# Narrow products of a hybrid decoder step placed side by side in TensorE's array

## The chip, the cores and the metric

The kernel runs on one core of a Trainium2 chip. The metric is the device time of one execution in microseconds (us). Engines are called as the profile calls them: PE is TensorE's matmul, PEld its weight load, DVE is VectorE, ACT is ScalarE, POOL is GpSimd, SP is SyncE, which issues most DMAs.

## What is computed

One inference step of a decoder layer for 1024 prompt tokens and for 32 new tokens (8 sequences of 4, each with 1024 past tokens). Cut to what the change touches:

```python
mod = silu(c) @ w_ada + b_ada                       # 9 conditions: the prompt's and the 8 sequences'
shift, scale, gate = split(mod, 3)
# indexer, new tokens: relu of each of 4 heads, weighted and summed over the heads
s = einsum('bqhd,bsd->bqhs', qi, ki); scores = einsum('bqhs,bqh->bqs', relu(s), w)
# retention of the prompt, in 8 chunks of 128 tokens, 8 heads of 64
scores = einsum('bihd,bjhd->bhij', q, k) * dmat
# output projection with the gate, residual and final norm
x = x + gate[:, None, :] * (merged @ w_out)
y = rms_norm(x, g_final)
```

All of it is in 32-bit floats. Products whose operands are plain float32 (F32) run as two passes of the array, so that the profile has two matmuls and two weight loads for each; products that are written as three terms (high, low) in float32r (F32R) run in one pass each.

## The kernel before

The kernel is one program of some 20,000 instructions without loops at run time. It is written with tiles; a planner orders the instructions of each engine by their priority (the order in which the program was written) and by a simulated timeline, and sets the waits. `issue_after` ties an instruction behind another one on its engine. The stages follow each other in time:

- Until 152 us: norms, modulation, the indexer's projections and scores. The new tokens' index scores end in the **index sums** (L822 to L826): for each half G of the sequences, `wsel[:, G]` (128 rows, 32 columns) is multiplied with `RL[G]` in two runs of 512 columns, and both G add up in one PSUM tile of 32 rows and 1024 columns. One ACT copy brings it to `SCS`, on which the search for the 256 best keys works.
- 152 to 516 us: **retention** (`pair`, for four pairs p of heads), its projections on PE, and on DVE and ACT the search (31 rounds, tied to the projections by `marks`). The products of keys and queries (L596 to L601) run for two groups g of four chunks. `two()` takes two PSUM tiles `pb` of the three that there are, one for each head i; head i uses rows 64i to 64i+63 of the array and all 128 columns, so that the products of two heads can run side by side.
- 516 to 700 us: scores of the new tokens against gathered keys (`past_scores`), beside the projections of keys and values.
- 700 to 817 us: the new tokens' values (`values`, gathers of 512 KB on POOL's queue, products L1100) beside, for p = 0 to 3, `silu_rows(p)` (a projection of 72 matmuls), `gates(12 + p)` (another) and **`gate_rows(p)`**: two loads from `w_ada`, 32 narrow matmuls in four column parts of the array (L212), an ACT copy to `ga`, a product with the 32 columns of `C_SEL` that adds up the four parts (L994), an ACT copy of 9 rows to `gr`, and a DMA of these to DRAM (`GD`). Loads of projection weights and of `w_ada` share the two buffers `ws` in turn; `project` takes the weights split before and begins with `prefetch` of the next: load, ACT cast to `wh` (L204), difference to `wl` on DVE or POOL (L205), each with two buffers as well. A `ws` buffer of projection weights is free after the split, one of `w_ada` after its L212.
- 817 to 972 us: attention of the prompt, filled up with the products of retention's rows (L1006 to L1008).
- 972 to 1023 us: merging, output j by output j; the new tokens' columns of each go to `MS` as high and low parts. `load_wo(0)` loads the four blocks of `w_out`'s first half into `wst` (4 buffers) and splits them.
- 1023 us to the end: **output projection**. `part(t, sl, ...)` takes one tile of 128 prompt tokens (t < 8), 24 F32R matmuls of 512 columns for each half of the outputs, or the 32 new tokens (t = 8): 16 F32R matmuls of 512 columns for each half, with 32 or 64 columns of the array used. The order is (8, 0, 1) first halves, then their second halves, then tiles 2 to 7 one by one; `final` norms a tile and writes it.

Of the kernel before, what the change touches and what calls it, by code (L numbers as in the profile page):

```python
# [117 lines left out]
def _hybrid_step(ctx, tc, A, outs, dbg):  # L118
# [406 lines left out]
    def pair(rp, RC, O, SD, p, rows):  # L525
# [70 lines left out]
        for g in (0, 1):  # L596
            px = two()
            together([lambda c=c, i=i: nc.tensor.matmul(px[i][:, 128 * c:128 * c + 128],
                                                        kT[head[i], 512 * g + 128 * c:512 * g + 128 * c + 128],
                                                        qT[head[i], 512 * g + 128 * c:512 * g + 128 * c + 128], start=True, stop=True)  # L600
                      for c in range(4) for i in (0, 1)])  # L601
# [94 lines left out]
    with ExitStack() as s1:  # L696
# [4 lines left out]
        with ExitStack() as s2:  # L701
# [120 lines left out]
            for G in (0, 1):  # L822
                for n0 in (0, 512):
                    nc.tensor.matmul(x[:NS, n0:n0 + 512], wsel[:, G], RL[G][:, n0:n0 + 512], start=(G == 0), stop=(G == 1))
                nc.tensor.matmul(xn[:NS, :NS], wsel[:, G], RL[G][:, PAST:], start=(G == 0), stop=(G == 1))
            nc.scalar.copy(SCS[:, :PAST], x[:NS])  # L826
# [159 lines left out]
    def gate_rows(tl, p):  # L986
# [4 lines left out]
        ga = tl.tile([128, 256], F32, name="ga", bufs=1)  # L991
        nc.scalar.copy(ga, x[:, :256])
        x = pj()
        nc.tensor.matmul(x[:NS, :256], C[:, C_SEL:C_SEL + 32], ga, start=True, stop=True)  # L994
        gr = tl.tile([9, 256], F32, name="gr", bufs=1)
        nc.scalar.copy(gr, x[:9, :256])
        (nc.scalar if p == 3 else nc.sync).dma_start(GD[:, 256 * p:256 * p + 256], gr)
# [144 lines left out]
    yrh, yrl = rows_in(rm, YR)  # L1142
    for p in range(4):
        silu_rows(tl, p)
        gates(tl, (12 + p,))
        gate_rows(tl, p)
    nc.sync.dma_start(zs, by_pair(ZD))
    nc.vector.tensor_tensor(YS, YS, zs, op=OP.mult)
    tl_.close()
    hs_.close()  # L1150
# [172 lines left out]
    MS = fp.tile([128, KT, 2, NS], F32R, name="MS")  # L1323
    WO = [[fp.tile([128, KT, 512], F32R, name=f"wo{a}0") for a in "hl"]]

    def load_wo(q, js):

        for j in js:
            w = fp.tile([128, 4, 256], F32, name="wst", bufs=4)
            g, c = divmod(j, 2)  # L1330
            nc.sync.dma_start(w, A["w_out"][0][512 * g:512 * g + 512, 512 * q + 256 * c:512 * q + 256 * c + 256].rearrange("(k p) f -> p k f", p=128))
            h, l = [a[:, 4 * g:4 * g + 4, 256 * c:256 * c + 256] for a in WO[q]]
# [3 lines left out]
    for n_, j in enumerate(line):  # L1336
# [4 lines left out]
        def use_a(c, sl, x):  # L1341
# [4 lines left out]
            if c == 2:  # L1346
                parts((MS[:, j, 0], MS[:, j, 1]), t[:, T:])
# [25 lines left out]
    def part(t, sl, i, xo, xr, sv):  # L1373
# [14 lines left out]
        else:  # L1388
            for k in range(KT):
                if k > 0:  # L1390
                    nc.tensor.matmul(x[:NS], MS[:, k - 1, 0], wl[:, k - 1], start=False, stop=False)
                    if k == KT - 1:
                        nc.tensor.matmul(x[:NS], MS[:, k, 0], wl[:, k], start=False, stop=False)
                nc.tensor.matmul(x[:2 * NS], MS[:, k].rearrange("p a c -> p (a c)"), wh[:, k], start=(k == 0), stop=(k == KT - 1))
            nc.scalar.copy(g, x[NS:2 * NS])
            nc.vector.tensor_tensor(g, g, x[:NS], op=OP.add)
# [16 lines left out]
    for ts in ((8, 0, 1), (2,), (3,), (4,), (5,), (6,), (7,)):  # L1413
        cuts = halves if ts != (7,) else [slice(0, 512), slice(512, 768), slice(768, 1024)]
        tiles = {}
        for i, sl in enumerate(cuts):
            for t in ts:
                if i == 0:
                    xo, xr = op_.tile([128, D], F32, name="xo", bufs=3), urow()[:, :D]
                    tiles[t] = xo, xr, op_.tile([128, 4], F32, name="sv", bufs=4)  # L1420

                    with tc.issue_after(asked[line[-1]].ins):
                        nc.sync.dma_start(*((xr, xp[128 * t:128 * t + 128]) if t < 8 else (xr[:NS], xs)))
# [26 lines left out]
```

## Time and profile before

| | us |
|---|---|
| time, median of 3 runs | 1127.78 (1127.6 to 1127.87) |
| the profiled execution's own time | 1127.94 |
| span in the profile | 1126.2 |
| PE busy (share of the span) | 1087.8 (97%) |
| PEld busy | 988.8 (88%) |
| DVE busy | 678.6 (60%) |
| ACT busy | 472.4 (42%) |
| POOL busy | 226.6 (20%) |
| DMA moved, mean | 183.51 MB, 163 GB/s |

The span is the time from the first to the last instruction of the program in one profiled execution; that execution's own time is 1.7 us longer. Matmuls are pipelined: the next one starts before the last one's end, so a group's cost is read from starts, or from the busy time of the group, not from the mean duration of one. A time that follows "idle before" is time in which the engine waited, with the event that ended it.

### The profile page before, as it was taken

What the parts mean: (1) busy time and instruction counts of PE and PEld (TensorE: products, weight loads), DVE (VectorE), ACT (ScalarE), POOL (GpSimd) and SP (SyncE); (2) the same over time, 40 slices, a digit from 0 to 9 for tenths busy, and PEclk for the clock granted to TensorE, in tenths of its full rate; (3) what the DMA queues carried; (4) which work ended last, traced back from release to release, by engine and by line L of the source; (5) the groups of instructions that cost most, each with busy time, mean ns of one, the idle gap of its engine ahead of it and who ended that gap; (6) DMA issues with size and microseconds to landing.
All of it is one profiled execution on the core that took longest, in us unless ns stands there. A gap on an engine that the chain in (4) does not pass through costs nothing.

```text
span 1126.2 us, 20190 instructions
## 1 busy us (share of the span) xinstructions
PE 1087.8 (97%) x7978; PEld 988.8 (88%) x7978; DVE 678.6 (60%) x1649; ACT 472.4 (42%) x914; POOL 226.6 (20%) x194
## 2 busy tenths in 40 slices
PE   6989999999999999989999999989999999999997
PEld 5779889899999999989999999767889888898886
DVE  6775348698878969996222222201367777488645
ACT  6574345455554644232343323211335666343111
POOL 0012006114321211022321212232013333100000
PEclk9999999999999999999999999999999999999999
DMA  9933335155243434414877666586897511456321
GB/s 311 234 90 95 101 98 152 45 172 142 78 151 111 134 92 152 134 42 136 294 240 242 186 203 204 185 299 225 272 328 274 185 61 41 151 159 230 121 90 56
DMA packets 153909, 183.51 MB, mean 163 GB/s; under 512 B 18565, under 2 KB 124749, under 8 KB 152726
## 3 DMA queue, kind: packets, MB, share of 16 engines
q1 hardware_dynamic: 143718, 145.96, 41.6%
q0 software_dynamic: 9856, 35.66, 9.6%
q8 instruction: 63, 1.03, 0.4%
q10 hardware_dynamic: 240, 0.61, 0.1%
q14 instruction: 32, 0.26, 0.1%
HBM read 137.23 MB, written 41.17 MB: 158 GB/s over the span
## 4 chain that ended last, share of the span: by engine, by line
PE 83%; DVE 8%; DMA 5%; issue 2%; ACT 1%; SPq 1%; DVEq 0%; ACTq 0%
PE pj L218 15%; PE pj L219 15%; PE pj L220 15%; PE po L1229 3%; PE pj L1006 3%; PE pj L1007 3%; PE pj L1008 3%; PE pj L1384 3%; PE pj L1385 3%; PE pj L1386 3%; PE str L1072 3%; PE tr L1212 2%; PE lg L1190 2%; DMA x<-in_w_ada 1%; PE sx L1051 1%
## 5 line engine op out<-in xcount | busy, mean ns | idle before, releaser
L218 PE MATMUL pj<-hh,wh 128*128 128x352 f32 (+1 forms) x1168 | 383.2, 328 | 1.6 <-DVE qs L724 1.1
L219 PE MATMUL pj<-hl,wh 128*128 128x352 f32 (+1 forms) x1168 | 378.8, 324 | 0.0
L220 PE MATMUL pj<-hh,wl 128*128 128x352 f32 (+1 forms) x1168 | 378.6, 324 | 0.0
L218 PEld LDWEIGHTS pj<-hh,wh 128*128 128x128 f32 x1168 | 219.8, 188 | 11.4 <-issue 8.5
L219 PEld LDWEIGHTS pj<-hl,wh 128*128 128x128 f32 x1168 | 220.3, 189 | 3.4 <-issue 2.5
L220 PEld LDWEIGHTS pj<-hh,wl 128*128 128x128 f32 x1168 | 219.7, 188 | 1.5 <-issue 0.8
L842 DVE TENSOR_SCALAR_CACHE_REDUCE eq<-sc,cand 128x896 bf16<-128x896 f32 (+4 forms) x155 | 135.8, 876 | 2.6
L204 ACT CAST wh<-ws 128x1024 fp32r<-128x1024 f32 (+1 forms) x65 | 61.0, 941 | 128.0 <-PE pj L219 73.1
L205 DVE TENSOR_TENSOR wl<-ws,wh 128x1024 fp32r<-128x1024 f32 (+1 forms) x48 | 58.2, 1213 | 62.5 <-ACT wh L204 62.4
L1199 POOL TENSOR_SCALAR lg<-lg,st 128x1024 f32<-128x1024 f32 (+7 forms) x64 | 47.9, 754 | 119.4 <-DVE st L1198 106.5
L205 POOL TENSOR_TENSOR wl<-ws,wh 128x1024 fp32r<-128x1024 f32 x17 | 41.7, 2450 | 143.2 <-ACT wh L204 121.0
L1197 ACT ACTIVATE lg<-lg,st 128x1024 f32<-128x1024 f32 (+7 forms) x64 | 49.5, 774 | 29.9 <-DVE st L1196 27.8
L1074 DVE COPY kt<-str 128x512 f32<-128x512 f32 x32 | 22.1, 690 | 62.1 <-PE str L1072 58.4
L1384 PE MATMUL pj<-woh,MH 128*128 128x512 f32 (+1 forms) x136 | 51.2, 377 | 0.0
L1385 PE MATMUL pj<-wol,MH 128*128 128x512 f32 (+1 forms) x136 | 51.2, 377 | 0.0
L1386 PE MATMUL pj<-woh,ML 128*128 128x512 f32 (+1 forms) x136 | 51.2, 377 | 0.0
L1042 POOL DMA_INDIRECT kv<-in_cache_k,idx x32 | 30.1, 941 | 99.2 <-PE str L1072 82.0
L690 ACT ACTIVATE raw<-pj 128x352 f32<-128x352 f32 x48 | 22.2, 463 | 65.0 <-PE pj L220 59.7
L1042 POOL DMA_INDIRECT kv<-in_cache_v,idx x32 | 30.1, 941 | 81.5 <-PE sx L1100 46.5
L1212 PE MATMUL tr<-C,lg 128*128 128x128 f32 x288 | 44.6, 276 | 1.5 <-ACT pT L1214 0.6
L1074 ACT COPY kt<-str 128x512 f32<-128x512 f32 x32 | 18.8, 588 | 60.9 <-PE str L1072 51.7
L1212 PEld LDWEIGHTS tr<-C,lg 128*128 128x128 f32 x288 | 33.6, 140 | 10.2 <-ACT pT L1214 2.5
(352 smaller groups left out, 1977.4 us busy)
## 6 DMA issues: line engine op xcount, KB each, us to landing
ws<-in_w_in SPq DMA_DIRECT2D x51, 512.0 KB
rot<-in_rot SPq DMA_DIRECT2D x8, 1056.0 KB
x<-in_w_ada SPq DMA_DIRECT2D x16, 512.0 KB
TG<-raw SPq DMA_DIRECT2D x15, 528.0 KB
u<-TG SPq DMA_DIRECT2D x8, 528.0 KB
t<-TG SPq DMA_DIRECT2D x8, 528.0 KB
x<-in_x_prompt SPq DMA_DIRECT2D x8, 512.0 KB
qdh<-raw SPq DMA_DIRECT2D x8, 512.0 KB
```

Of the source, the lines that this page charges most:

```text
L204: nc.scalar.copy(wh[:, :, :n], ws[:, :, :n])
L205: (nc.vector if k == 4 or len(order) % 3 else nc.gpsimd).tensor_sub(wl[:, :, :n], ws[:, :, :n], f32(wh[:, :, :n]))
L218: nc.tensor.matmul(p, wh[:, k], HH[k][:, sl], start=(k == 0), stop=False)
L219: nc.tensor.matmul(p, wh[:, k], HL[k][:, sl], start=False, stop=False)
L220: nc.tensor.matmul(p, wl[:, k], HH[k][:, sl], start=False, stop=(k == KT - 1))
L842: nc.vector.tensor_scalar(junk[:n, :W], sc, thr[:n, j:j + 1], 0.0, op0=op, op1=OP.add, accum_out=cnt[:n, j:j + 1])
L1042: nc.gpsimd.indirect_dma_start(out=t.rearrange("p s c -> p (s c)"), out_offset=None, in_=cache.rearrange("g (r s) h d -> (g r) (s h d)", s ...
L1197: nc.scalar.activation(l, l, AF.Exp, bias=st[:, 2:3], scale=0.125, accum_out=st[:, 3:4])
L1212: nc.tensor.transpose(x[:, 128 * (j - j0):128 * (j - j0) + 128], lg[:, j % 2, 128 * (j // 2):128 * (j // 2) + 128], ident)
L1384: nc.tensor.matmul(x, MH[:, k, tk], wh[:, k], start=(k == 0), stop=False)
L1385: nc.tensor.matmul(x, MH[:, k, tk], wl[:, k], start=False, stop=False)
L1386: nc.tensor.matmul(x, ML[:, k, tk], wh[:, k], start=False, stop=(k == KT - 1))
```

## The change

It has four parts, and the order around two of them.

- Products of keys and queries: each head's product of a chunk is cut into two, for the keys 0 to 63 and 64 to 127 of the chunk, so that each uses 64 rows and 64 columns of the array. There are 16 products for a group instead of 8, written in an order in which four next to each other use four different places.
- Index sums: the second run of 512 columns goes to PSUM rows 32 to 63, and so to other columns of the array than the first; the copy to `SCS` becomes two.
- Gate sums: `gate_rows(p)` ends with the copy into its 256 columns of `GA`. Once all four are there, `gate_sums` runs the four products to four column parts, one copy of 128 rows, and four DMAs from ACT's queue. `gate_rows(p)` comes before `gates(12 + p)` instead of after it, and `gate_sums` before `gates(15)`.
- New tokens' output projection: `MS` holds plain F32, and the products use the unsplit weights in `wst`: for each half of the outputs 16 F32 products of 256 columns in place of the 16 F32R ones of 512, four of them to four column parts (each for one fourth of the inputs' rows), then a copy of 128 rows and two additions of parts and one of sums. Tile 8 leaves the head of the output projection: its second half comes after the second halves of tiles 0 to 2, then the four blocks of the first half of `w_out` are loaded again without a split (`load_wo(0, range(4), False)`, 2 MB), and its first half follows tile 4.

```diff
-            together([lambda c=c, i=i: nc.tensor.matmul(px[i][:, 128 * c:128 * c + 128],
-                                                        kT[head[i], 512 * g + 128 * c:512 * g + 128 * c + 128],
-                                                        qT[head[i], 512 * g + 128 * c:512 * g + 128 * c + 128], start=True, stop=True)
-                      for c in range(4) for i in (0, 1)])
+            together([lambda c=c, i=i, o=o: nc.tensor.matmul(px[i][o:o + 64, 128 * c:128 * c + 128],
+                                                             kT[head[i], 512 * g + 128 * c + o:512 * g + 128 * c + o + 64],
+                                                             qT[head[i], 512 * g + 128 * c:512 * g + 128 * c + 128], start=True, stop=True)
+                      for c in range(4) for i, o in ((0, 0), (1, 64), (0, 64), (1, 0))])
...
-                for n0 in (0, 512):
-                    nc.tensor.matmul(x[:NS, n0:n0 + 512], wsel[:, G], RL[G][:, n0:n0 + 512], start=(G == 0), stop=(G == 1))
+                for o, n0 in ((0, 0), (32, 512)):
+                    nc.tensor.matmul(x[o:o + NS, n0:n0 + 512], wsel[:, G], RL[G][:, n0:n0 + 512], start=(G == 0), stop=(G == 1))
...
-            nc.scalar.copy(SCS[:, :PAST], x[:NS])
+            for o, n0 in ((0, 0), (32, 512)):
+                nc.scalar.copy(SCS[:, n0:n0 + 512], x[o:o + NS, n0:n0 + 512])
...
-        ga = tl.tile([128, 256], F32, name="ga", bufs=1)
-        nc.scalar.copy(ga, x[:, :256])
+        nc.scalar.copy(GA[:, 256 * p:256 * p + 256], x[:, :256])
+
+    def gate_sums():
+
         x = pj()
-        nc.tensor.matmul(x[:NS, :256], C[:, C_SEL:C_SEL + 32], ga, start=True, stop=True)
-        gr = tl.tile([9, 256], F32, name="gr", bufs=1)
-        nc.scalar.copy(gr, x[:9, :256])
-        (nc.scalar if p == 3 else nc.sync).dma_start(GD[:, 256 * p:256 * p + 256], gr)
+        for p in range(4):
+            nc.tensor.matmul(x[32 * p:32 * p + 32, :256], C[:, C_SEL:C_SEL + 32], GA[:, 256 * p:256 * p + 256], start=True, stop=True)
+        gr = gq.tile([128, 256], F32, name="gr", bufs=1)
+        nc.scalar.copy(gr, x[:, :256])
+        for p in range(4):
+            nc.scalar.dma_start(GD[:, 256 * p:256 * p + 256], gr[32 * p:32 * p + 9])
...
         silu_rows(tl, p)
+        gate_rows(tl, p)
+        if p == 3:
+            gate_sums()
         gates(tl, (12 + p,))
-        gate_rows(tl, p)
...
-    MS = fp.tile([128, KT, 2, NS], F32R, name="MS")
+    MS = fp.tile([128, KT, NS], F32, name="MS")
...
-            for k in range(KT):
-                if k > 0:
-                    nc.tensor.matmul(x[:NS], MS[:, k - 1, 0], wl[:, k - 1], start=False, stop=False)
-                    if k == KT - 1:
-                        nc.tensor.matmul(x[:NS], MS[:, k, 0], wl[:, k], start=False, stop=False)
-                nc.tensor.matmul(x[:2 * NS], MS[:, k].rearrange("p a c -> p (a c)"), wh[:, k], start=(k == 0), stop=(k == KT - 1))
-            nc.scalar.copy(g, x[NS:2 * NS])
-            nc.vector.tensor_tensor(g, g, x[:NS], op=OP.add)
+
+            for j in range(4):
+                h, c = divmod(j, 2)
+                for k in range(4):
+                    nc.tensor.matmul(x[32 * k:32 * k + 32, 256 * c:256 * c + 256], MS[:, 4 * h + k], whole[q, j][:, k], start=(j == 0), stop=(j == 3))
+            four = op_.tile([128, 512], F32, name="four", bufs=1)
+            nc.scalar.copy(four, x)
+            for o, dst in ((64, four[64:96]), (0, g)):
+                nc.vector.tensor_tensor(dst, four[o:o + 32], four[o + 32:o + 64], op=OP.add)
+            nc.vector.tensor_tensor(g, g, four[64:96], op=OP.add)
...
-    for ts in ((8, 0, 1), (2,), (3,), (4,), (5,), (6,), (7,)):
+    for ts in ((0, 1, 2), (3,), (4,), (5,), (6,), (7,)):
...
+        if ts == (0, 1, 2):
+            take(8)
+            part(8, halves[1], 0, *tiles[8])
+            load_wo(0, range(4), False)
+        if ts == (4,):
+            part(8, halves[0], 1, *tiles[8])
+            final(8, 2, *tiles[8])
```

## Rows read from the trace of the kernel before

**Rows 1.** The page: busy time, share of the span and instructions of the engines, and the clock granted to TensorE in 40 equal slices (9 stands for 90% or more of full speed).

```profile
PE 1087.8 (97%) x7978; PEld 988.8 (88%) x7978; DVE 678.6 (60%) x1649; ACT 472.4 (42%) x914; POOL 226.6 (20%) x194
...
PEclk9999999999999999999999999999999999999999
```

**Rows 2.** The windows view: busy time (and instructions) of each engine in a stretch of the span, then granted clock, share of the DMA engines' time, GB/s. The stretches are two of retention and search, one of the new tokens' values and the gates, and the output projection.

```profile
300.00:452.00 152.00, 152.00 (x1118) 145.91 (x1117) 124.30 (x327) 75.98 (x132) 28.40 (x14) 1.00 0.40 121
452.00:516.00 64.00, 60.05 (x465) 56.80 (x464) 60.85 (x89) 17.56 (x33) 7.48 (x4) 1.00 0.29 78
...
700.00:817.00 117.00, 109.44 (x887) 89.80 (x885) 19.74 (x35) 26.90 (x51) 29.26 (x28) 0.99 0.73 246
...
1043.00:1122.00 79.00, 74.97 (x354) 62.87 (x352) 46.29 (x133) 11.15 (x32) 0.00 (x0) 1.00 0.24 89
```

**Rows 3.** The timeline of all engines at the index sums of the first four sequences (L824): start and length in us, engine, line, operation, tiles, shape. PE is the matmul, PEld its weight load.

```profile
138.55 1.90 PE L824 MATMUL pl<-rl,wsel 128*32 128x512 f32 x4
139.00 0.11 PEld L824 LDWEIGHTS pl<-rl,wsel 128*32 128x32 f32 x1 [0.32 <-issue]
139.43 0.11 PEld L824 LDWEIGHTS pl<-rl,wsel 128*32 128x32 f32 x1 [0.32 <-issue]
...
140.38 0.43 PE L218 MATMUL pj<-hh,wh 128*128 128x352 f32 x1
```

**Rows 4.** Groups of instructions by line and shape: count, busy time of the group in us, mean of one in ns, idle time before them. L1100 and L1051 are the new tokens' values and scores, four sequences to the four 32-column parts of the array.

```profile
L1100 PE MATMUL sx<-kv,PS 128*32 128x512 f32 x128 | 15.4, 598 | 2.3 <-DMA kv<-in_cache_v,idx 2.3
...
L1051 PE MATMUL sx<-kt,QB 128*32 128x256 f32 x256 | 15.5, 382 | 0.0
...
L1051 PEld LDWEIGHTS sx<-kt,QB 128*32 128x32 f32 x256 | 7.5, 109 | 5.8 <-issue 1.5 <-DVE wl L205 0.2
```

**Rows 5.** The chain of work that ended last, in order of time: start, share of the chain, what. One call of the scores (L1051, 16 products) and the transposes behind it.

```profile
684.84 1.86 PE sx L1051 x32
686.70 1.03 PE str L1072 x8
...
691.23 0.87 PE str L1072 x8
```

**Rows 6.** The timeline of TensorE at the retention's products of queries and keys of the first head pair (L598; 64 rows by 128 columns of the array each).

```profile
199.52 0.71 PE L598 MATMUL pb<-qrT,krT 64*128 64x128 f32 x6
...
200.37 1.61 PE L598 MATMUL pb<-qrT,krT 64*128 64x128 f32 x18
...
204.78 1.16 PE L598 MATMUL pb<-qrT,krT 64*128 64x128 f32 x8
```

**Rows 7.** The timeline of TensorE at one call of the index products (L811), 64 rows by 32 columns of the array each, eight of them for eight places.

```profile
131.92 1.09 PE L811 MATMUL pl<-kp,QF 64*32 64x512 f32 x16
```

**Rows 8.** The timeline of TensorE at three of the four gate sums (L994); in square brackets the idle time before a row and what ended it.

```profile
746.54 0.59 PE L994 MATMUL pj<-ga,C 128*32 128x256 f32 x2
747.07 0.43 PE L218 MATMUL pj<-hh,wh 128*128 128x352 f32 x1
...
787.23 0.62 PE L994 MATMUL pj<-ga,C 128*32 128x256 f32 x2 [0.48 <-ACT ga L992]
...
816.37 0.62 PE L994 MATMUL pj<-ga,C 128*32 128x256 f32 x2 [0.49 <-ACT ga L992]
816.92 0.43 PE L1006 MATMUL pj<-rh,wh 128*128 128x352 f32 x1
```

**Rows 9.** The timeline of ScalarE in the stage of values and gates: two casts of projection weights and the copy behind the second.

```profile
716.36 1.05 ACT L204 CAST wh<-ws 128x1024 fp32r<-128x1024 f32 x1 [4.16 <-DMA ws<-in_w_in]
...
758.50 1.04 ACT L204 CAST wh<-ws 128x1024 fp32r<-128x1024 f32 x1 [10.96 <-DMA ws<-in_w_in]
759.45 0.20 ACT L1112 COPY ys<-str 128x64 f32<-128x64 f32 x1
```

**Rows 10.** The timeline of TensorE in the same place.

```profile
759.71 0.77 PE L1093 MATMUL str<-C,LG 128*128 128x128 f32 x5 [3.75 <-ACT ys L1112]
...
761.28 0.66 PE L218 MATMUL pj<-hh,wh 128*128 128x352 f32 x1 [0.48 <-DVE raw L982]
```

**Rows 11.** The windows view there; the count in brackets behind the first number is the matmuls of the stretch.

```profile
762.00:764.00 2.00, 2.00 (x8) 2.00 (x8) 0.04 (x1) 0.00 (x0) 0.00 (x0) 0.50 0.86 253
764.00:766.00 2.00, 2.00 (x13) 2.00 (x13) 0.00 (x0) 0.00 (x0) 0.00 (x0) 0.98 0.00 0
```

**Rows 12.** The timeline of SyncE's DMA queue in that stage: issues of projection weights (ws from w_in) and of the gate's weights (ws from w_ada), x2 where two were issued next to each other.

```profile
710.06 1.47 SPq L198 DMA_DIRECT2D ws<-in_w_in  x2
...
730.45 0.37 SPq L198 DMA_DIRECT2D ws<-in_w_ada  x1
...
743.51 1.41 SPq L198 DMA_DIRECT2D ws<-in_w_in  x2
```

**Rows 13.** The timeline of GpSimd: the first and the last of the eight value gathers of one burst (the six between them stand 1.2 to 2.9 us apart).

```profile
740.36 0.93 POOL L1042 DMA_INDIRECT kv<-in_cache_v,idx  x1 [5.11 <-PE sx L1100]
...
750.68 0.94 POOL L1042 DMA_INDIRECT kv<-in_cache_v,idx  x1 [0.31 <-issue]
```

**Rows 14.** The timeline of TensorE at the new tokens' second half of the output projection: the first of its 16 matmuls, all in one run, and the prompt's matmul behind them.

```profile
1037.61 0.39 PE L1394 MATMUL pj<-woh,MS 128*64 128x512 f32 x1
...
1041.30 0.40 PE L1384 MATMUL pj<-woh,MH 128*128 128x512 f32 x1
```

**Rows 15.** Who waited for whom on SyncE's DMA queue between 795 and 830 us: in all, times, longest.

```profile
SPq L1167 <- DMA TG<-raw: 7.8, 1, 7.8
```

More of the change, by code (lines that the diff above doesn't have):

```diff
@@ L1142, in _hybrid_step @@
     yrh, yrl = rows_in(rm, YR)
+    gq_ = ExitStack()
+    gq = gq_.enter_context(tc.tile_pool(name="gq", bufs=1, reuse_waits="tile"))
+    GA = gq.tile([128, D], F32, name="ga")
     for p in range(4):
         silu_rows(tl, p)
+        gate_rows(tl, p)
+        if p == 3:
+            gate_sums()
         gates(tl, (12 + p,))
-        gate_rows(tl, p)
     nc.sync.dma_start(zs, by_pair(ZD))
@@ L1149, in _hybrid_step @@
     tl_.close()
+    gq_.close()
     hs_.close()
@@ L1322, in _hybrid_step, with load_wo @@
     MH, ML = [fp.tile([128, KT, T], F32R, name=n) for n in ("MH", "ML")]
-    MS = fp.tile([128, KT, 2, NS], F32R, name="MS")
+    MS = fp.tile([128, KT, NS], F32, name="MS")
     WO = [[fp.tile([128, KT, 512], F32R, name=f"wo{a}0") for a in "hl"]]
-    def load_wo(q, js):
+    whole = {}
+    def load_wo(q, js, split=True):
         for j in js:
-            w = fp.tile([128, 4, 256], F32, name="wst", bufs=4)
+            w = whole[q, j] = fp.tile([128, 4, 256], F32, name="wst", bufs=4)
             g, c = divmod(j, 2)
             nc.sync.dma_start(w, A["w_out"][0][512 * g:512 * g + 512, 512 * q + 256 * c:512 * q + 256 * c + 256].rearrange("(k p) f -> p k f", p=128))
+            if not split:
+                continue
             h, l = [a[:, 4 * g:4 * g + 4, 256 * c:256 * c + 256] for a in WO[q]]
@@ L1346, in use_a @@
             if c == 2:
-                parts((MS[:, j, 0], MS[:, j, 1]), t[:, T:])
+                nc.scalar.copy(MS[:, j], t[:, T:])
         for _ in out_weights(A["w_pa"][0], use_a, j, 4, yah, yal):
@@ L1412, in _hybrid_step, with take @@
     halves = [slice(0, 512), slice(512, 1024)]
-    for ts in ((8, 0, 1), (2,), (3,), (4,), (5,), (6,), (7,)):
+    tiles = {}
+    def take(t):
+        xo, xr = op_.tile([128, D], F32, name="xo", bufs=3), urow()[:, :D]
+        tiles[t] = xo, xr, op_.tile([128, 4], F32, name="sv", bufs=4)
+        with tc.issue_after(asked[line[-1]].ins):
+            nc.sync.dma_start(*((xr, xp[128 * t:128 * t + 128]) if t < 8 else (xr[:NS], xs)))
+    for ts in ((0, 1, 2), (3,), (4,), (5,), (6,), (7,)):
         cuts = halves if ts != (7,) else [slice(0, 512), slice(512, 768), slice(768, 1024)]
-        tiles = {}
         for i, sl in enumerate(cuts):
@@ L1418, in _hybrid_step @@
                 if i == 0:
[L1419 to L1423, printed above, removed]
+                    take(t)
                 part(t, sl, i, *tiles[t])
```

## The prediction

> **What bounds the kernel now.** I read the page first: PE is busy 97% of the span at full clock [rows 1], so the question for every edit is whether it takes time out of PE's row of instructions, and whether PE then waits for something else. The windows view by stage says where that can happen [rows 2]. From 300 to 452 us PE is busy all the time and DVE has 28 us idle in 152; time that PE saves before that passes through. From 452 to 516 DVE is the bound (60.85 of 64 us, PE idles 4): nothing that PE saves inside it counts, but DVE's work there starts from PE's projections and so moves with them. From 700 to 817 PE idles 7.6 us, and the DMA engines move 246 GB/s. From 1043 on PE is busy 74.97 of 79 us, and the 4 us left are the last tile's ending, which no edit touches: what is saved there is saved in full.
>
> **Index sums.** Two runs of 512 columns, two passes each, follow one another. The loads show the beat: 139.00, 139.43, so 0.43 us for a pass; the whole visit of one G takes from 138.55 to 140.38, 1.83 us [rows 3]. After the change the runs have different columns of the array. That such products run beside each other the trace shows elsewhere: 128 passes of the same shape in four column parts take 15.4 us, 0.12 each instead of 0.43 [rows 4]. So two passes of four go, 0.86 us for each G: **1.72 us** for both. ACT copies twice 512 columns instead of once 1024; ACT is busy half of the next stage [rows 2], and the search behind it has DVE's 28 us of idle time. Cover gone, this would cost some 0.2 us once.
>
> **Products of queries and keys.** For the first group, two heads' tiles are free, and the 64-row products already run in pairs that fill the array; for the second group the third `pb` buffer serves one head and the other waits, so that they run alone: 6 + 18 + 8 passes in 0.71, 1.61 and 1.16 us [rows 6]. The change doubles the products and halves each. Four at a time fill the array as two did; a head alone has two halves side by side where it had one pass of the same length. The count of beats is the same, so I take **0**. Bounds: eight places at a time are shown (16 passes of 512 columns in 1.09 us) [rows 7], though not this shape. If four run only as two, group one takes 8 more beats of 0.107 us (a fourth of the 0.43 for 512 columns), 0.9 us for each of the three pairs that are not under DVE: 2.7 us lost. If the sequence of starts gets tighter, at most the slow starts (1.16 us for 8 passes, 0.145 instead of 0.107) go: 0.3 us for each, 0.9 us gained. I take the middle because the eight-place row is the nearest.
>
> **Gate sums.** Each of the four visits costs 0.53 to 0.55 us from its start to the next one's, and the last two wait another 0.48 and 0.49 us for the ACT copy [rows 8]; the one not in these rows is taken like the first. That is 0.53 + 0.53 + 1.03 + 1.04 = 3.13 us. After the change one visit of two beats remains, and a wait for the last copy: 1.04 us; if `gates(15)` is drawn in front of it, 0.55. Gain **2.1 us**, up to 2.6. ACT loses three small copies and gets three more DMA issues; it is busy 26.90 of 117 us there [rows 2]. SP loses three issues, which stood among the weight loads.
>
> **Output projection of the new tokens.** The 16 matmuls of a half take from 1037.61 to 1041.30, 0.231 us each [rows 14]; both halves 7.38 us, all on PE's path. The new form is that of the scores, 16 products of 256 columns in four column parts, 32 passes: 1.86 us, and the work behind such a visit starts slowly (1.03 us where eight transposes take 0.87) [rows 5]. Two visits of 2.02 us: gain **3.34 us**. What is moved: the order (0, 1, 2) puts 17 us of first halves (72 matmuls) ahead of the second half's weights instead of 15 (64), so those have more time. The second visit needs four more blocks, 2 MB, issued on SP after the first one's release of `wst`; SP's queue has the outputs of tiles 0 to 2 and the rows for tiles 3 and 4 in it, and two tiles (some 22 us, 96 matmuls of 0.231) to do it. The DMA engines are busy 24% of that stretch [rows 2]: covered; without the cover PE would wait, in order, in front of the visit. The longer tail of copy and additions lies on ACT (11 of 79 us) and DVE (46 of 79); four PSUM banks stand between them and PE.
>
> By the Trainium skill ("TensorE: Matmul & The Clock Gate", Part 3, "What overlaps and what doesn't") a weight load overlaps matmuls in flight only where the row group differs, and parts by columns have the same rows; by that rule this edit loses (the last rival). The scores' row speaks against it here: 256 loads of 109 ns belong to 256 passes that took 15.5 us, 61 ns each [rows 4].
>
> **The stall that stands in the way.** Between 755 and 764 us PE waits 3.75 us for a copy on ACT and 0.48 us for DVE [rows 10]. ACT's row tells why: the copy stands behind a cast that waited 10.96 us for weights [rows 9], issued at 743.51 [rows 12] in the middle of eight gathers from 740 to 751 [rows 13]; they landed after 15.0 us, where those issued at 710.06 needed 6.3 [rows 9, 12]. Afterwards the granted clock is 0.50, the lower of the two levels, and 8 matmuls run in 2 us instead of 13 [rows 11]: another 1.1 us lost between 761.3 and 764. The stall costs 5.3 us. The change moves just these loads: they wait for L212 to free `ws`, and L212 of p now follows `silu_rows(p)`, one projection (72 matmuls, 11 us) earlier. The loads of 743 would go out near 728, between bursts, and those for the next p near 759, behind the burst. I take it that this stall goes. In its place `w_ada`'s second block for p = 2, which follows the cast at the end of `gates(13)`, goes out near 744.5, into the burst; with 15.0 us to land it comes at 759.5, when PE, after 72 matmuls, a values visit of 1.9 us [rows 4] and some transposes, wants it at about 758.5: 1.0 us lost (0 to 3.5). Last, SP stood 7.8 us behind the write of `gates(15)` [rows 15] before the attention's operands; the 2.1 us of `gate_rows(3)` that followed that projection now come ahead of it, so the operands come up to 2.1 us later against PE. Retention's products fill much of that; I take 0.8 us.
>
> **Sum.** 1.72 + 2.1 + 3.34 = 7.2 us of PE work, plus 5.3 for the stall, less 1.0 and 0.8: 10.7 us. The profiled execution took 1127.94 us (the median is 0.16 lower, which I neglect): **1117.2 us**. Its own bounds: down to 1112.9 with neither of the two waits (1.8), the sums' wait filled (0.5), the tighter products (0.9) and half of the 2.3 us that the values wait for gathers [rows 4]; up to 1122.4 with fours that run as twos (2.7) and the long wait for `w_ada` (2.5 more).
>
> **Rivals.**
> - *The stall only moves.* Another cast lands late with ACT's queue behind it. Then the work saved and the 0.8 remain: 1127.9 - 7.2 + 0.8 = 1121.5. For it: the planner places casts by its own time for a load, and three of them waited for DMA in this stage, the shown 4.16 and 10.96 us among them [rows 9]. Against it: the new places lie between bursts. 24%.
> - *The gathers become the bound.* 246 GB/s are moved from 700 to 817 [rows 2], and PE waited 2.3 us for gathers in the values [rows 4]. If PE's earlier arrival is all spent waiting for them, what was saved before 817 is lost, and only the output projection's 3.34 us remain: 1124.6. Against it: the DMA engines idle 27% of the stage. 12%.
> - *Slower: the gate's weights come late each time.* `w_ada`'s second block has one projection's time to land, 11 us and what lies between, and a wait for it stops PE itself, in order, and can bring the lower clock. If each of p = 1 to 3 meets a burst like that of 743, three stalls of 5.3 us stand against one: 1127.9 - 7.2 + 2 x 5.3 = 1131.3. It decides from three on; with two it is 1126.0. Against it: the old order had the same time for the same block (issued at 730.45, used by the L212 that freed the loads of 743.51 [rows 12]), and PE didn't wait for it in this stage. 8%.
> - *Weight loads of the column parts stop the matmuls.* If a load can't run beside a matmul in the same rows, a visit of the output projection takes 32 loads of 0.109 us [rows 4] and 8 beats of 0.215 (half of the 0.43), 5.2 us instead of 2.02: 6.4 us worse for two, the index sums gain nothing (1.72), and the gate sums only their waits (1.1 less): 1117.2 + 6.4 + 1.7 + 1.1 = 1126.4. The scores' rows exclude it [rows 4, 5]. 2%. It is what the skill's rule on loads, named above, would give.
>
> **How the numbers follow.** Forecast 53%, the rivals 24, 12, 8 and 2%, 1% for what I don't see. The range for 8 in 10 takes in most of the forecast, the moved stall and most of the gathers: 1113.5 to 1124.6. A difference of 0.2% (2.3 us) is about what a measurement of this kernel can tell from no change. Faster by that: the forecast, the moved stall and three quarters of the gathers, 0.86; slower by that: three quarters of the third and what I don't see, 0.07; within: the rest, 0.07.
>
> **What would show it.** Right: L824 with two passes for each visit's beat, a visit of 1.0 us; one L994 group with four starts a few ns apart; tile 8's two visits of 1.9 us; L598's passes for a pair unchanged in sum (3.5 us); no cast in ACT's row that waits 10 us with PE's L1093 behind it; the clock without its dip at 760. Wrong: a weight load or `w_ada` as the releaser of a PE wait of over 2 us after 700, a dip of the clock elsewhere, PE waiting for `wst` near 1080, or a shorter L598, which would mean that places count there after all.

## The result, and the profile after

The changed kernel takes 1124.26 us (median of 13 runs, 1120.92 to 1127.32) where the kernel before, run beside it, takes 1128.65 (13 runs, 1127.60 to 1130.87): ratio **0.9948, 95% interval 0.9938 to 0.9958**, a gain of 5.9 us (4.7 to 7.0) on 1128. The forecast was 1117.2, a gain of 10.7. The profiled execution took 1124.63 us (span 1122.8). Of the forecast's sum some 5 us are missing. The ratio is not the quotient of the two medians, which is 0.9961 (4.4 us) and lies outside the interval; so a difference of one microsecond between two such figures says little by itself. The profiled executions of the two kernels lie 3.3 us apart (1127.94 and 1124.63): the other 2.6 us of the measured gain stand in no trace.

The page, answering [rows 1]: PE's busy time is nearly the same with 160 instructions more. That row can't show the gain: a matmul at the lower clock is busy for longer, and the mean granted clock of this execution is 0.990 where it was 0.997.

```profile
PE 1087.0 (97%) x8138; PEld 990.2 (88%) x8138; DVE 682.7 (61%) x1645; ACT 471.1 (42%) x912; POOL 226.0 (20%) x194
```

The windows view of the changed kernel, answering [rows 2, 11]. From 1043 on PE's busy time fell from 74.97 to 71.41 us, although tile 8's two visits, which stood ahead of 1043 before, now lie in this stretch. From 700 to 817 it still idles 7.2 us, as before (7.6), and the granted clock is 0.97 where it was 0.99. Behind 782 us six matmuls run in 2 us at the lower level, where 14 run at full clock four microseconds later.

```profile
452.00:516.00 64.00, 60.06 (x491) 56.92 (x490) 61.26 (x88) 16.19 (x32) 7.46 (x5) 0.97 0.29 78
700.00:817.00 117.00, 109.80 (x867) 92.23 (x867) 21.43 (x36) 27.79 (x51) 28.91 (x28) 0.97 0.74 248
1043.00:1122.00 79.00, 71.41 (x384) 58.19 (x382) 50.34 (x139) 12.27 (x36) 0.00 (x0) 0.97 0.33 117
782.00:784.00 2.00, 1.73 (x6) 1.73 (x7) 1.11 (x1) 0.57 (x2) 0.00 (x0) 0.53 0.36 112
786.00:788.00 2.00, 2.00 (x14) 2.00 (x13) 0.00 (x0) 0.27 (x1) 0.00 (x0) 1.00 0.09 26
```

The timeline of TensorE in the changed kernel at the edits, answering [rows 3, 6, 8, 14]: an index visit with the matmul behind it, the products of the first pair, the one visit of the gate sums, and tile 8's second visit. The index visit takes 0.98 us to the next matmul (138.81 to 139.79) instead of 1.83; the gate sums are one visit of 0.57 with one wait of 0.49; tile 8's visit takes 1.87 us (1079.30 to 1081.17) instead of 3.69, without a wait for `wst`. The products' three pieces last 0.45, 1.75 and 1.09 us instead of 0.71, 1.61 and 1.16: 0.2 us less for a pair, with twice the passes.

```profile
138.81 1.05 PE L825 MATMUL pl<-rl,wsel 128*32 128x512 f32 x4
139.79 0.43 PE L218 MATMUL pj<-hh,wh 128*128 128x352 f32 x1
...
198.08 0.45 PE L599 MATMUL pb<-qrT,krT 64*64 64x128 f32 x8
...
198.68 1.75 PE L599 MATMUL pb<-qrT,krT 64*64 64x128 f32 x40
...
201.96 1.09 PE L599 MATMUL pb<-qrT,krT 64*64 64x128 f32 x16
...
803.75 0.64 PE L999 MATMUL pj<-ga,C 128*32 128x256 f32 x8 [0.49 <-ACT ga L993]
...
1079.30 1.93 PE L1409 MATMUL pj<-wst,MS 128*32 128x256 f32 x32
1081.17 0.50 PE L1400 MATMUL pj<-woh,MH 128*128 128x512 f32 x1
```

So the edits do on PE what was forecast. What is missing went in two places. (PE's lead, here and below, is the time by which the same matmul of the same product starts earlier than in the trace of the kernel before.) The first is from 700 to 817. The waits of TensorE there (690 to 820 us): in all, times, longest.

```profile
PE sx L1057 <- DVE kt L1080: 2.8, 1, 2.8
PE pj L218 <- ACT raw L691: 2.3, 1, 2.3
PE sx L1106 <- DMA kv<-in_cache_v,idx: 1.5, 1, 1.5
PE pj L999 <- ACT ga L993: 0.5, 1, 0.5
```

The old stall of 3.75 us at 756 [rows 10] is gone; two new ones stand in its place. ScalarE's timeline of the changed kernel, answering [rows 9]:

```profile
699.94 1.04 ACT L204 CAST wh<-ws 128x1024 fp32r<-128x1024 f32 x1 [4.28 <-DMA ws<-in_w_in]
700.89 0.46 ACT L691 ACTIVATE raw<-pj 128x352 f32<-128x352 f32 x1
...
780.81 1.04 ACT L204 CAST wh<-ws 128x1024 fp32r<-128x1024 f32 x1 [10.52 <-DMA ws<-in_w_in]
781.76 0.81 ACT L691 ACTIVATE raw<-pj 128x352 f32<-128x352 f32 x2
```

VectorE's timeline at the first of them; the copy that PE waits for stands behind the second half of the same weight split:

```profile
701.02 1.23 DVE L205 TENSOR_TENSOR wl<-ws,wh 128x1024 fp32r<-128x1024 f32 x1 [5.68 <-ACT wh L204]
702.16 0.68 DVE L1080 COPY kt<-str 128x512 f32<-128x512 f32 x1
```

SyncE's queue, answering [rows 12]: the loads behind these casts, issued 6.1 and 11.3 us before the casts could start. The first of them had gone out at 661.84 in the kernel before; in the new order two blocks of `w_ada` (661.26 and 679.74) stand ahead of it.

```profile
693.88 0.39 SPq L198 DMA_DIRECT2D ws<-in_w_in  x1
...
769.47 0.37 SPq L198 DMA_DIRECT2D ws<-in_w_in  x1
```

The second lies in a burst of gathers, answering [rows 13]; the first and the last of four on GpSimd:

```profile
767.78 0.94 POOL L1048 DMA_INDIRECT kv<-in_cache_v,idx  x1 [2.96 <-PE sx L1106]
...
771.51 0.94 POOL L1048 DMA_INDIRECT kv<-in_cache_v,idx  x1 [0.31 <-issue]
```

It is the old chain at two other places: a load that waited for L212 to free `ws`, a cast in ACT's order in front of evacuations (the copies that take PE's results out of PSUM), and PE behind these. Each time the granted clock is 0.50 for 3.4 us afterwards (703.6 to 707.0 and 782.1 to 785.5). Against the kernel before PE enters this stage 0.6 us early and leaves it 1.05 early (first matmul of retention's rows at 815.87 instead of 816.92): in this execution 0.4 us gained where 6.4 were forecast (2.1 + 5.3 - 1.0). The second place is 488 to 514 us, where PE's lead of 1.7 us falls to 0.7; the experiments tell why.

### The profile page after: what moved, and what is told of

It reads as the page before. It is cut to its first block, busy times and chain, and to the rows that moved or that the text cites. A ratio compares the mean times of both kernels' runs of the same rounds, so it can differ in the third digit from the quotient of the medians.

```text
span 1122.8 us, 20509 instructions
## 1 busy us (share of the span) xinstructions
PE 1087.0 (97%) x8138; PEld 990.2 (88%) x8138; DVE 682.7 (61%) x1645; ACT 471.1 (42%) x912; POOL 226.0 (20%) x194
## 3 DMA queue, kind: packets, MB, share of 16 engines
q8 instruction: 64, 1.05, 0.4%
## 4 chain that ended last, share of the span: by engine, by line
PE 84%; DVE 7%; DMA 5%; issue 2%; ACT 1%; SPq 1%; DVEq 0%; ACTq 0%
PE pj L218 15%; PE pj L220 15%; PE pj L219 15%; PE po L1241 3%; PE pj L1012 3%; PE pj L1014 3%; PE pj L1013 3%; PE pj L1400 3%; PE pj L1401 3%; PE pj L1402 3%; PE str L1078 2%; PE tr L1224 2%; PE lg L1202 2%; DMA ws<-in_w_in 2%; PE sx L1057 1%
## 5 line engine op out<-in xcount | busy, mean ns | idle before, releaser
L205 DVE TENSOR_TENSOR wl<-ws,wh 128x1024 fp32r<-128x1024 f32 (+1 forms) x48 | 54.7, 1139 | 60.8 <-ACT wh L204 60.1
```

The source lines that it names most:

```text
L205: (nc.vector if k == 4 or len(order) % 3 else nc.gpsimd).tensor_sub(wl[:, :, :n], ws[:, :, :n], f32(wh[:, :, :n]))
```

## Experiments

All times are ratios to the kernel before, run on the same chip beside each; 0.0010 is 1.13 us.

**One part alone.** Each kernel is the kernel before with these lines of the change and what belongs to them.

```diff
 # e1_outproj: load_wo, MS, tile 8
+                    nc.tensor.matmul(x[32 * k:32 * k + 32, 256 * c:256 * c + 256], MS[:, 4 * h + k], whole[q, j][:, k], ...)
 # e2_index
+                for o, n0 in ((0, 0), (32, 512)):
+                    nc.tensor.matmul(x[o:o + NS, n0:n0 + 512], wsel[:, G], ...)
 # e3_gates: gate_rows ahead of gates, one gate_sums
+        gate_rows(tl, p)
+        if p == 3:
+            gate_sums()
 # e4_products
+                      for c in range(4) for i, o in ((0, 0), (1, 64), (0, 64), (1, 0))])
```

> The kernel before with the change's output projection of the new tokens alone. Theory (the work terms of the prediction are right, and what is missing was given back between 700 and 817 us): both visits of tile 8 last 1.9 us as in the whole change, PE ends 3.3 us earlier, ratio 0.9971, about 1125.3 us against 1128.65; the stall at 756 to 764 us stays as it was. Rival (the reordered loads and the longer tail of ACT and DVE work cost something that the whole change's trace hides): less than 2.5 us gained, ratio over 0.9978.

Measured 0.9975 (0.9962 to 0.9987), 2.8 us; in the trace PE ends 3.17 us earlier and both visits last 1.9 us. The theory holds; the interval excludes neither.

> The kernel before with the change's index sums alone. Theory (a gain ahead of the stage that DVE bounds passes through it, and the 1.0 us that the whole change lost at 494 to 502 us came with another edit's order of work): two visits of 1.0 us in place of 1.83, and 1.7 us less at the end, ratio 0.9985, about 1127.0 us. Rival (the stage that DVE bounds takes the gain back): 0.7 us or less, ratio 0.9994 or more, and a PE wait of about 3 us for DVE near 494 us with a fall of the granted clock behind it.

Measured 0.9988 (0.9978 to 0.9999), 1.4 us. In the trace PE is 0.20 us late ahead of the two visits and 1.50 early behind them, 1.70 us in all, and keeps that lead up to 700; the wait near 495 is 2.11 us (2.13 before). The stage that DVE bounds takes nothing back: its work starts from PE's projections, as the prediction had said. The stage of the values does: the lead falls there from 1.5 to 0.5 us, most of it in a wait of 1.40 us for ACT's copy ahead of a gate sum (0.48 before).

> The kernel before with the change's gate sums and their new place alone. Theory (the gate sums save their 2 us, but a stall behind a weight cast that stands in ACT's order ahead of a late load only moves, and the attention's operands cost 0.8): between 0 and 2 us gained, ratio 0.998 to 1.000, and in the trace at least one PE wait of over 2 us between 700 and 817 us whose chain goes back to a cast that waits for its load, with a fall of the granted clock behind it. What the prediction had said of this part alone: 2.1 + 5.3 - 1.8 = 5.6 us gained, ratio 0.995. Rival (the gathers are the bound of this stage): no stall behind a cast, PE waits for gathers in the values, and no gain, ratio 0.9995 to 1.0005.

Measured 0.9970 (0.9957 to 0.9982), 3.4 us: more than the theory's 0 to 2, less than the prediction's 5.6. Its trace has the two stalls of the changed kernel (2.7 at 701.5, 1.7 at 781.2). They wait 4.4 us together where the old stall waited 4.2, so they cost no less. What PE gains in this stage of the trace, 2.6 us, is mostly the sums' 2.1, with shorter waits for gathers beside them (1.0 us instead of 2.3); 0.7 is lost again in the attention. So the edit is worth something although the stall has only moved.

> The kernel before with the change's products of queries and keys alone. Theory (the whole change's trace shows 0.2 us less for a pair, four pairs, of which two lie where DVE is not the bound): 0.3 to 0.8 us gained, ratio 0.9993 to 0.9997. Prediction: nothing, ratio 1.000. Rival (the four places side by side, or the order of DVE's work that goes with them, bring the wait and the fall of the clock at 494 to 502 us): slower by 0.5 to 1.5 us, ratio 1.0005 to 1.0013, with that wait in the trace.

Measured 1.0017 (1.0002 to 1.0031), **1.9 us slower**: the rival. The size is loose: the quotient of the medians is 1.0007. In the trace PE gains 0.3 us up to 480 us and loses 1.15 between 488 and 516. In the profiled execution a longer stretch at the lower clock behind the old stall (6.8 us instead of 3.4 near 761) adds to it.

Their sum is 2.8 + 1.4 + 3.4 - 1.9 = 5.7 us, against 5.9 for the whole: the parts add up, within intervals of over 1 us each.

**The products' loss.** The first kernel undoes the edit, the second does so in the last pair alone.

```diff
 # e5_no_products: the changed kernel with L598 as before
 # e8_last_old
+            m, places = (64, ((0, 0), (1, 64), (0, 64), (1, 0))) if p < 3 else (128, ((0, 0), (1, 0)))
```

> The changed kernel with the products of queries and keys in their old form, all else changed. Theory (the edit's order of work lets PE reach the wait for DVE near 494 us seven projection matmuls earlier, 3.06 us of waiting instead of 2.13, and the lower granted clock behind it costs what the edit alone was measured to cost): 1 to 2 us less than the changed kernel, ratio to the kernel before 0.993 to 0.994; the wait near 494 is 2.1 us. Rival (a fall of the clock in this stage is chance and DVE bounds the stage anyway): as the changed kernel, ratio 0.9948.

Measured 0.9937 (0.9922 to 0.9952): 1.2 us below the changed kernel's 0.9948, the wait 2.12. It is on the theory's side and agrees with e4, but its interval takes in 0.9948.

> The changed kernel with the old form of the products in the last pair only. In this kernel's order of work PE has 21 projection matmuls ahead of the products that wait for DVE, as in the changed kernel, where the kernel before has 28. Theory (the order makes the wait, not the four places): a wait of about 3 us near 494 us stays, with the old form behind it, and the time is the changed kernel's, ratio 0.9945 to 0.9955. Rival (the form itself makes the wait): a wait of 2.1 us and 1 to 2 us less, ratio 0.993 to 0.994.

Measured 0.9934 (0.9921 to 0.9947), and the wait is 2.96 us. Neither theory fits: the wait is the theory's and the time the rival's. The time alone decides little: the interval overlaps the changed kernel's, and in both traces PE also gains on the changed kernel from 700 to 817 (2.9 us in e5, 2.3 in e8; the second wait there is 1.5 us in both instead of 2.3, with no lower clock behind it). What happens between 488 and 520 the traces show: the changed kernel loses 1.0 us of PE's lead there, e5 and e8 nothing. Here is what differs. TensorE's groups from the products to the end of the last pair's retention, first in the kernel before (488.7 to 515.7), then in the changed one (487.0 to 513.8), then in e8_last_old (487.0 to 513.8):

```profile
L219 PE MATMUL pj<-hl,wh 128*128 128x352 f32 x22 | 7.4, 336 | 0.0
L218 PE MATMUL pj<-hh,wh 128*128 128x352 f32 x22 | 7.2, 327 | 0.0
L220 PE MATMUL pj<-hh,wl 128*128 128x352 f32 x22 | 7.2, 327 | 0.0
```

```profile
L218 PE MATMUL pj<-hh,wh 128*128 128x352 f32 x20 | 7.5, 373 | 0.0
L220 PE MATMUL pj<-hh,wl 128*128 128x352 f32 x19 | 7.0, 368 | 0.0
L219 PE MATMUL pj<-hl,wh 128*128 128x352 f32 x19 | 6.8, 355 | 0.0
L599 PE MATMUL pb<-qrT,krT 64*64 64x128 f32 x64 | 3.1, 274 | 3.1 <-DVE tmp L605 3.1
```

```profile
L218 PE MATMUL pj<-hh,wh 128*128 128x352 f32 x22 | 8.0, 364 | 0.0
L219 PE MATMUL pj<-hl,wh 128*128 128x352 f32 x21 | 7.4, 352 | 0.0
L220 PE MATMUL pj<-hh,wl 128*128 128x352 f32 x21 | 7.3, 349 | 0.0
L600 PE MATMUL pb<-qrT,krT 64*128 64x128 f32 x32 | 3.5, 293 | 3.0 <-DVE tmp L606 3.0
```

And the windows view of the same stretches, in the changed kernel and in e8_last_old:

```profile
487.00:513.80 26.80, 22.86 (x254) 20.27 (x252) 26.00 (x44) 7.75 (x15) 0.00 (x0) 0.94 0.08 22
```

```profile
487.00:513.80 26.80, 23.84 (x228) 21.35 (x226) 25.92 (x45) 7.71 (x15) 0.00 (x0) 0.94 0.09 22
```

DVE is busy 26 of 26.8 us and sets the stretch's length in all of them (27.0 before). What counts is how many projection matmuls stand in it in PE's order: 66 before, 58 in the changed kernel, 64 in e8_last_old, 58 in e4_products, 66 in e5_no_products. The rest is done later, where PE is the bound, at 0.16 us each: 8 x 0.16 = 1.28 us for e4 (1.15 lost), 6 x 0.16 = 0.96 between the changed kernel and e8_last_old (0.97 in the trace at 518 us). At a clock of 0.94 the stretch takes 26.8 us, at 1.00 (before) 27.0, so these 3.4 us at the lower level cost nothing here. A longer stretch does cost: e3_gates has the same 66 matmuls in the same order as the kernel before, but the lower level from 499.4 to 506.2, and PE comes out 0.70 us later. That window in the kernel before, then in e3_gates:

```profile
499.40:506.20 6.80, 5.82 (x41) 5.41 (x40) 6.80 (x11) 2.76 (x3) 0.00 (x0) 1.00 0.04 8
```

```profile
499.40:506.20 6.80, 6.80 (x26) 6.58 (x25) 6.80 (x11) 2.27 (x2) 0.00 (x0) 0.50 0.04 7
```

The kernel's order of work, in which the new products come with fewer projections around them, makes the loss; why the planner orders them so, no run tells.

**The stalls from 700 on.** First, buffers of their own for `w_ada`'s blocks, in the changed kernel and in the kernel before:

```diff
-            w = wload(wp, A["w_ada"][0], 2 * D + 256 * p + 128 * o, 128)
+            w = wload(gq, A["w_ada"][0], 2 * D + 256 * p + 128 * o, 128)
```

> The changed kernel with w_ada's blocks of the gate in two buffers of their own (8 KB of a partition more), so that no load of w_in waits for an L212 and none is issued late. Theory (the PE waits of 2.79 us at 700 and 2.31 us at 780 us come from weight casts that stand in ACT's order ahead of a load issued late): both waits and the falls of the clock behind them are gone, 4 to 7 us less than the changed kernel, ratio to the kernel before 0.989 to 0.992. Rival (the gathers are the bound between 700 and 817): PE waits for value gathers in their place, at most 1.5 us gained, ratio 0.9935 or more.

> The kernel before with w_ada's blocks in two buffers of their own and nothing else. Theory (the stall of 756 to 764 us comes from the same cause: loads of w_in that wait for L212): it is gone, 4 to 6 us less than before, ratio 0.9947 to 0.9965, without any of the change. Rival (a stall only moves to another cast): less than 2 us, ratio over 0.998.

Measured 1.0098 (1.0082 to 1.0113) and 1.0055 (1.0040 to 1.0071): **slower by 11 and 6 us**, a clear miss of theory and rival both. The planner, free of the buffers' ties, drew the values forward (the first two visits stand 24 and 39 groups of three projection matmuls earlier in e6_own, 14 and 24 in e7_before_own); the waits of the two kernels (690 to 820 us), the first two of each:

```profile
PE pj L218 <- ACT ga L993: 5.2, 2, 4.7
PE sx L1106 <- DMA kv<-in_cache_v,idx: 4.4, 1, 4.4
```

```profile
PE sx L1100 <- DMA kv<-in_cache_v,idx: 5.3, 2, 4.2
PE pj L994 <- issue: 3.9, 1, 3.9
```

The granted clock from 696 to 820 is 0.92 in both. The edit changed the order of work with the buffers, so it doesn't tell the theories apart. A gather that PE reaches too early costs as much there as the old cast (4.4 and 4.2 us), and the clock's loss comes on top; what held up ACT's copy ahead of the gate sum in e6_own (4.7 us) and the gate sum in e7_before_own (3.9), the traces don't name.

Second, the cast alone: in the program loads, buffers and gathers stay, and for the last eight weight loads the cast goes behind the second evacuation in ACT's order.

```diff
-        prefetch()
+        prefetch(1 if len(order) <= 8 else None)
...
             use(c, p)
+            if c == HOLD and held:
+                f1, ws = held.pop()
+                with tc.issue_after(last_on(mybir.EngineType.Activation)):
+                    split.append((f1, wsplit(wp, ws, 128)))
```

> The kernel before with the same hold of the weight casts and nothing of the change. Theory: the stall of 756 to 764 us goes, with the fall of the clock behind it, 3 to 5.3 us less than before, ratio 0.9953 to 0.9973. Rival one (the gathers bound this stage): waits for gathers instead, ratio 0.9985 to 1.001. Rival two (the held cast comes too late): slower, ratio over 1.001.

Measured **0.9961** (0.9945 to 0.9976), 4.4 us: the theory. The cast that answers to the second of [rows 9] runs at 763.65 without a wait, and what is left of TensorE's waits there is

```profile
PE pj L1004 <- ACT ga L1002: 1.4, 3, 0.5
PE sx L1110 <- DMA kv<-in_cache_v,idx: 1.2, 2, 1.0
```

with a granted clock of 1.00 from 696 to 820 us. From 690 to 817 PE's lead rises by 4.6 us. The planner moved other work with the cast: the loads go out at 749.35 instead of 743.51, and the gathers fall into two groups around 738 and 748. But the loads are still late (the cast runs 14.3 us after their issue), they still go out among gathers, and PE doesn't wait. So the old stall was worth about what the prediction said (5.3; 4.4 measured), and its cause, the cast's place, is shown, as far as one edit that moves other work too can show it.

> The changed kernel, in which from 585 us on each weight cast follows the second evacuation of the projection in progress in ACT's order, instead of standing ahead of it; loads, buffers and gathers as they were. Theory (the stalls of the changed kernel at 700 and 780 us come from casts that wait for a late load with evacuations behind them): no PE wait of over 1 us for ACT or DVE between 696 and 817, both falls of the clock there gone, 3 to 6 us less than the changed kernel, ratio to the kernel before 0.9895 to 0.992. Rival one (the gathers bound this stage, as the two runs with buffers of their own make likely): PE waits for value gathers instead, within 1.5 us of the changed kernel, ratio 0.9935 to 0.996. Rival two (the held cast comes too late for its own projection): PE waits in front of a projection for the weights, ratio over 0.996.

Measured 0.9999 (0.9983 to 1.0015): in the changed kernel the same hold costs 5.8 us. No cast of `w_in` holds PE for long any more between 700 and 817, but this does (690 to 820 us):

```profile
PE sx L1116 <- DMA kv<-in_cache_v,idx: 4.5, 3, 2.8
PE pj L1009 <- ACT ga L1003: 1.8, 1, 1.8
PE pj L212 <- DMA ws<-in_w_ada: 1.6, 1, 1.6
```

By its ratio this is rival two, though PE waits for `w_ada` and not for a projection's weights; the gathers of rival one come on top (4.5 us instead of 1.5). The held cast keeps its `ws` buffer longer, so the last block of `w_ada`, which in the new order is wanted one projection sooner, is issued at 798.26, right when GpSimd's half of the split ends (795.86 + 2.37), and PE wants it at 800.75. The loads of retention's weights go out behind it, and a cast that waits 1.1 us for one of them stands in front of the copy for the last gate sum (the 1.8 us). Behind it the clock is 0.50 from 803.6 to 810.4. In the profiled executions PE falls 3.5 us behind the changed kernel up to 817: 2.0 of them here, 1.2 already at 583, where a copy on ACT waits 4.5 us for the DMA that reads its buffer. So the changed order is tight on both sides: early casts stall on their loads, late casts keep the next load back. That the two new stalls come from their casts is thus read from the trace alone; no run took them out and gained by it.

```diff
 # e12_sums_old_order: e3_gates, but
         silu_rows(tl, p)
-        gate_rows(tl, p)
-        if p == 3:
-            gate_sums()
         gates(tl, (12 + p,))
+        gate_rows(tl, p)
+    gate_sums()
```

> The kernel before with the four gate sums made one, but gate_rows of p still after gates(12+p), so that no weight load is moved by it. Theory (the sums themselves save some 2 us, and what the gate edit gains beyond that comes from its new order): 1.5 to 2.5 us gained, ratio 0.9978 to 0.9987, and the stall of 756 us stays. Rival (the saving of the sums is hidden in waits of this stage and all of the gate edit's 3.4 us are its new order): under 0.7 us, ratio over 0.9994.

Measured 0.9988 (0.9978 to 0.9998), 1.4 us, between the two. Its interval overlaps that of e3, so that the new order adds to the sums is not shown; in the traces PE gains 3.1 us from 700 to 817 with the old order and 2.6 with the new. The stall of 756 didn't stay: without the sums' small copies the order shifts, and a wait of 3.1 us stands at 715.4, again behind a cast:

```profile
716.48 1.04 ACT L204 CAST wh<-ws 128x1024 fp32r<-128x1024 f32 x1 [2.09 <-DMA ws<-in_w_in]
717.43 0.58 ACT L1098 COPY PS<-str 128x512 f32<-128x512 f32 x1
```

**The parts that help, together.** The kernel before with the hold, the index sums and the output projection:

> The kernel before with the hold of the weight casts, and of the change only the index sums and the output projection; products, gate sums and the place of gate_rows as before. Theory (these parts add up, since each lies where PE is the bound): 0.9961 for the hold, 0.0025 less for the projection and 0.0012 less for the index sums, ratio 0.9924, from 0.991 to 0.9935, less than the changed kernel's 0.9948; two index visits of 1.0 us, two visits of tile 8 of 1.9 us, no PE wait of over 1.5 us for ACT or DVE between 700 and 817. Rival (an arrival 1.7 us earlier in this stage brings another stall, since its places are chance): ratio 0.9945 or more, with a new wait of over 2 us between 700 and 817.

Measured **0.9928** (0.9910 to 0.9946), 8.1 us: the theory. Its longest wait for ACT or DVE from 700 to 817 is 1.2 us. Its trace is no such clean sum: PE's lead rises by 1.7 us in this stage, not by the 4.6 of the hold alone, with the lower clock from 751.0 to 754.4. The interval overlaps the changed kernel's, so that it is the faster of the two is likely, not shown.

## Why the prediction was right and where not

The sign was right, and 1124.26 lies inside the range, 0.34 us below its upper end; the gain was 5.9 us and not 10.7. That it lies inside is in part luck: the range reached so far only to take in the rival of the gathers, which didn't come.

- **Index sums, 1.72:** 1.70 in the trace, 1.4 measured alone. Right, with its reason that a gain ahead of the DVE stage passes through; that a microsecond of it can go in the stage of the values (e2_index) it didn't price.
- **Output projection, 3.34:** 3.17 and 3.26 in the traces, 2.8 (1.5 to 4.3) measured alone. Right, cover included: no wait for `wst`. The Trainium skill's rule of the last rival ("TensorE: Matmul & The Clock Gate", Part 3, "What overlaps and what doesn't": a weight load overlaps matmuls in flight only where the row group differs) gives, as the prediction estimated it, 5.2 us for a visit, and the trace shows 1.87: 32 loads and passes in 58 ns each, all with the same rows. It doesn't hold for these column parts.
- **Products, 0:** on PE's own row right (0.2 us less for a pair), in the time wrong: 1.9 us slower (0.2 to 3.5), of which the traces show 1.0 to 1.15 between 488 and 520. The step that failed is "the count of beats is the same, so I take 0". It priced the products and not the order of work around them, although the prediction itself named the stage where DVE is the bound. There, a matmul is free as long as it is drawn into the stage, and eight of them no longer were.
- **Gate sums, 2.1, and "I take it that this stall goes", 5.3:** the second is the step that failed. That stall went, and with the cause given: casts in ACT's order in front of evacuations (e11 shows it: 4.4 us). But the change doesn't remove the cause. It moves the loads, and two other casts took its place. The loads that the prediction put near 728 and 759, outside the bursts, went out at 734.83 and 769.47, both among gathers; and the stall at 700 it didn't look for at all. This is the rival "the stall only moves", which gave 1121.5, a gain of 6.4. That it comes so near the measured 5.9 is luck too: it has 1.3 for the gate edit and nothing for the products, and they measured 3.4 (2.0 to 4.9, where the forecast had 5.6) and -1.9. The sums in the old order measured 1.4; on PE's row they save the 2.1 (one visit of 0.57 and one wait of 0.49 for the 3.13 before).
- **w_ada's wait, 1.0:** didn't come in the changed kernel. In e9_hold it did: 1.6 us, with a late issue as described.
- **Attention's operands, 0.8:** PE's lead falls from 1.05 to 0.30 us there, and by 0.7 in e3, e5 and e8 as well. Right in size, but not by the reason given: the operands' loads went out earlier (811.63 and 819.34 instead of 813.35 and 822.63), and no wait of PE there is for a DMA. The longest is one of 0.48 us for GpSimd's part of the scores (0.09 before); what else changed, no run tells.

By parts measured alone the missing 5 us are 2.2 for the gate edit, 1.9 for the products, and some 0.9 that lies within the intervals of the other two.

## What to carry to other kernels

A stall that goes because a load moves is not a gain until the cause (here a cast in an engine's order ahead of work that isn't its own) is gone: look for the next place where the same three conditions meet, and price it. In a stage that another engine bounds, count the fill work that stands in it: an edit that costs its own engine nothing can still push that work out to where it counts. Change a buffer and the planned order changes with it; hold one instruction back by itself to test a cause, and look in the trace at what moved with it.

## What the runs showed of the hardware

- The granted clock falls to the lower of its two levels (1.2 of 2.4 GHz) behind some PE waits and not behind others like them. After the same wait of 2.1 us near 498, with the same work of the last pair ahead of it, it stayed 1.00 in the kernel before, in e1_outproj, e2_index and e5_no_products; it was 0.50 for 3.4 us in e11_before_hold and e12_sums_old_order, and from 499.4 to 506.2 in e3_gates. Where PE is the bound more than a third of such a stretch is lost (8 matmuls in 2 us instead of 13 [rows 11]); in the stage that DVE bounds 3.4 us cost nothing (e11, e12: PE's lead is the same on both sides) and 6.8 us cost 0.70 (e3). The spread of one kernel goes with it in part: the fastest of the 13 runs after has a mean clock of 0.996 and the slowest 0.991, but a run of 1121.66 has 0.991 too.
- Four products of 64 rows and 64 columns start 7 ns apart, with twice the instructions of two of 128 columns. The beat is the same (109 ns for four passes, 105 to 112 for two); the 0.2 us that a pair of heads gains are at the head of each run, where the second set starts 0.14 to 0.16 us after the first instead of 0.21.
